# Stick-breaking attention: the scan's input moves from PSUM to SBUF, and the PSUM banks are dealt out anew

## The chip, the cores and the metric

The kernel runs on one core of a Trainium2 chip. The metric is the device time of one execution in microseconds (us). TensorE (PE) multiplies matrices and writes PSUM, which has eight banks of 128 partitions x 512 fp32 values; VectorE (DVE), ScalarE (ACT) and GpSimd (POOL) work element by element; SyncE (SP) issues most of the DMAs. Each engine takes its instructions in the order in which they were written.

## The reference

One decoder block for 2048 tokens of width 1024: conditioning, a projection, eight attention heads of 64 channels beside four pooling groups, an output projection and a feed-forward layer. The change lies in the attention:

```python
z = q @ k.T / sqrt(64)                     # scores, strictly causal (s < t)
logw[t, s] = logsigmoid(z[t, s]) + sum_{s < j < t} logsigmoid(-z[t, j])
out = exp(logw) @ v
```

The kernel doesn't form logarithms. The weight of key s is sigmoid(z_s) times the product of sigmoid(-z_j) over the later keys j, so each row of scores needs two sigmoids and one running product from right to left.

## The kernel before, in words

The kernel has four stages on the time axis of the profile: conditioning and input projection (to about 325 us), attention (about 325 to 862 us, with the rest of the input projection woven in), output projection with the second norm (to about 1060 us), and the feed-forward layer. Engine orders of the first two stages are written out by hand: the order of the calls in the source is the order in each engine's queue.

**The steps of the attention.** The work goes by units (h, tb, sc): head h, a block of 512 queries tb, a block of 512 keys sc, from sc = tb (the diagonal block) down to 0. A unit has four steps, i = 0 to 3, each with 128 queries on the partitions and L keys along the free axis: L = 512 off the diagonal, 128, 256, 384 and 512 on it. There are 80 units and 320 steps: 192 off the diagonal, and 128 on it. In pass n of the main loop the engines get, in this order:

- `weights_step` of step n (L792 to 808). PE puts the scores into a PSUM bank z (L801, L802, and L804 for the mask). ACT writes sigmoid(z) to an SBUF tile sg (L806), and then sigmoid(-z) over the scores in the same PSUM bank (L807).
- `scan_step` of step n-1 (L810 to 823). POOL writes the column at the right end of an SBUF tile pr: 1.0 on the diagonal (L815), else column 0 of the pr of the same i in the unit before (L817). DVE runs the scan from right to left (L818): first input z in PSUM, second input sg (with operation bypass, so that its values don't count), start value the same column of the older pr. POOL multiplies sg by pr shifted by one key and gets the weights w (L821).
- `values_step` (L839 to 855): two products of turned weights with values, into a PSUM bank av.
- `turn_step` of step n-7 (L825 to 838). PE turns four 128x128 blocks of w into a PSUM bank wt (L833); ACT rounds it to wth (L59), DVE subtracts for the rest wtl (L60).
- some pieces of the remaining projection (`pieces`): three products of 512 columns each and now and then an eviction, a split of weights by ACT and POOL, a running sum by POOL.

**Buffers.** PSUM has three banks z, two wt, two av and one mm (for the woven projection). In SBUF pr has 6 buffers (four of them hold the start values of the next unit), sg 5, w 11. `z_ps`, `t_ps`, `av_ps` hand out the banks (L153 to 155), each group in turn.

Of the kernel before, what the change touches and what calls it, by code (L numbers as in the profile page):

```python
# [9 lines left out]
F32 = mybir.dt.float32  # L10
F32R = mybir.dt.float32r
AF = mybir.ActivationFunctionType
ALU = mybir.AluOpType
# [4 lines left out]
P = 128  # L18
# [10 lines left out]
TB = 512  # L29
# [3 lines left out]
NEG = -1e30  # L33
LAG = 2
OFF = 7
ZB, WB = 3, 2
FT = {"sr": 4, "p1": 1, "u2": 2, "u3": 2, "u4": 1, "cu": 2, "s": 6, "gs": 3, "tr": 4, "gf": 1}
PAIRS, HELD = 6, 4
RB = PAIRS - 1
# [5 lines left out]
def block_kernel(ctx, tc, x, c, w_cond, b_cond, g_mix_pre, g_mix_post, w_in, w_pool,  # L45
                 pool_scale, w_out, g_ffn_pre, g_ffn_post, w_gate, w_up, w_down, out):
    nc = tc.nc
# [17 lines left out]
    def mm3(ps, terms, first=True, last=True):  # L65

        n = len(terms)
        for i, ((lh, ll), (rh, rl)) in enumerate(terms):
            nc.tensor.matmul(ps, lh, rh, start=first and i == 0, stop=False)  # L69
            nc.tensor.matmul(ps, lh, rl, start=False, stop=False)  # L70
            nc.tensor.matmul(ps, ll, rh, start=False, stop=last and i == n - 1)  # L71

    def open_pool(stack, name, bufs=1, side=None):
        kw = {"side": side} if side else {}
        return stack.enter_context(tc.tile_pool(name=name, bufs=bufs, reuse_waits="tile", **kw))
# [68 lines left out]
    def psum(tag, bufs, name):  # L144
        return psp.tile([P, TB], F32, tag=tag, bufs=bufs, name=name)

    turn = [0]

    def mm_ps(name, alone=False):
        turn[0] += 1  # L150
        return z_ps(name) if turn[0] % 2 and not alone else psum("mm", 1, name)

    z_ps = lambda name: psum("z", ZB, name)  # L153
    t_ps = lambda name: psum("wt", WB, name)
    av_ps = lambda name: psum("av", 2, name)

    ident_r = c1.tile([P, P], F32R, tag="ident_r", name="ident_r")
    nc.vector.tensor_copy(ident_r, ident)
# [2 lines left out]
    one = ones[:, 0:1]  # L161
# [149 lines left out]
    def tokens(tb, k, cols=slice(0, TB)):  # L311
        if tb == 1:
            both = ht[1][k // HK]
            return both[:, 0, k % HK, cols], both[:, 1, k % HK, cols]
        return ht[tb][0][:, k, cols], ht[tb][1][:, k, cols]
# [111 lines left out]
    def pieces(th, chunks, tasks, loaded):  # L427
# [11 lines left out]
        for i, (n, tb) in enumerate(tasks):  # L439
            kind, m = chunks[n]  # L440
            ps = mm_ps(f"{kind}{m}_{tb}", attending)
            for k in range(KC):
                if k == 0 and th and todo.get(KC * i, [(0, 0)])[0][1] is None:
                    loaded[todo[KC * i][0][0]] = chunk_load(chunks[todo[KC * i][0][0]], th)
                    todo[KC * i].pop(0)
                w = loaded[n]
                mm3(ps, [((w[1][:, k, :], w[2][:, k, :]), tokens(tb, k))],
                    first=k == 0, last=k == KC - 1)
                for c, part in todo.get(KC * i + k, ()):
                    if part is None:  # L450
                        loaded[c] = chunk_load(chunks[c], th)
                    else:
                        chunk_split(loaded[c], part)
                if k == KC - 1:
                    take_chunk(chunks[n], tb, ps)
                run_small()
                yield
            if th == 1:
                yield

    def take_chunk(chunk, tb, ps):
        kind, m = chunk
        if kind == "u":
            ops = pool_ops(tb, ps, m)
            urgent.append(next(ops))
            small.append(ops)
        else:
            urgent.append(lambda: store_qk(tb, ps, (qd if kind == "q" else kd)[m], f"{kind}{m}"))

    def v_pieces(wvs, pool):  # L470
        for tb in (1, 0, 2, 3):
            for j in range(4):
                ps = mm_ps(f"v{tb}_{j}")
                cols = slice(j * P, (j + 1) * P)
                for k in range(KC):
                    mm3(ps, [(tokens(tb, k, cols), (wvs[0][:, k, :], wvs[1][:, k, :]))],
                        first=k == 0, last=k == KC - 1)
                    if k == KC - 1:
                        urgent.append(lambda a=(tb, j, ps, pool): store_v(*a))
                    run_small()  # L480
                    yield
# [119 lines left out]
        modulate(1, kc, pt)  # L601

    first_ps = {}
    first_banks = {(0, 0): ("mm", 1), (0, 1): ("av", 2), (1, 1): ("av", 2)}

    def first_products(n, tb, *ks):
        if (n, tb) not in first_ps:
            first_ps[n, tb] = psum(*first_banks.get((n, tb), ("z", ZB)), f"first{n}_{tb}")
        ps = first_ps[n, tb]
        for k in ks:  # L610
            mm3(ps, [((loaded[n][1][:, k, :], loaded[n][2][:, k, :]), tokens(tb, k))], first=k == 0, last=k == KC - 1)
        if ks[-1] == KC - 1:
            take_chunk(chunks[n], tb, ps)
# [15 lines left out]
    chunk_split(loaded[0], 3)  # L629
    modulate0(0, 1)  # L630
    first_products(0, 0, 0, 1)
    scales = [normed_rows(1, 0, early1[0]), normed_rows(1, 1, early1[1])]
    chunk_split(loaded[1], 0)
    chunk_split(loaded[1], 1)
    modulate0(2, 3)
    scales += [normed_rows(1, 2, early1[2]), normed_rows(1, 3, early1[3])]
    first_products(1, 0, 0, 1)
    first_products(0, 0, 2, 3)
    chunk_split(loaded[1], 2)
    chunk_split(loaded[1], 3)  # L640
# [129 lines left out]
    att = open_pool(ph1, "att", bufs=2)  # L770
# [14 lines left out]
        nc.sync.dma_start(raw(vt), vd[tb][:, h, :].rearrange("(b p) e -> p b e", p=P))  # L785
        return qt

    qts, prevs, avs, wss = {}, {}, {}, {}

    scans = []  # L790

    def weights_step(u, i):  # L792

        h, tb, sc = u
        diag = sc == tb
        kt, qt = kv[h, sc][0], qts[h, tb]
        L = (i + 1) * P if diag else TB
        nm = f"{h}_{tb}_{sc}_{i}"
        z = z_ps(f"z{nm}")
        keys = kt[:, 0:L]  # L800
        nc.tensor.matmul(z[:, 0:L], qt[:, 0, i * P:(i + 1) * P], keys, start=True, stop=False)  # L801
        nc.tensor.matmul(z[:, 0:L], qt[:, 1, i * P:(i + 1) * P], keys, start=False, stop=not diag)  # L802
        if diag:
            nc.tensor.matmul(z[:, i * P:L], ident_r, neg_r, start=False, stop=True)  # L804
        sg = att.tile([P, TB], F32, tag="sg", bufs=5, name=f"sg{nm}")
        nc.scalar.activation(sg[:, 0:L], z[:, 0:L], AF.Sigmoid, scale=0.125)  # L806
        nc.scalar.activation(z[:, 0:L], z[:, 0:L], AF.Sigmoid, scale=-0.125)  # L807
        scans.append((u, i, z, sg, L, nm))

    def scan_step(u, i, z, sg, L, nm):  # L810

        diag = u[1] == u[2]
        pr = att.tile([P, TB + 1], F32, tag="pr", bufs=6, name=f"pr{nm}")
        if diag:
            nc.gpsimd.memset(pr[:, L:L + 1], 1.0)  # L815
        else:
            nc.gpsimd.tensor_copy(pr[:, L:L + 1], prevs[i][:, 0:1])  # L817
        nc.vector.tensor_tensor_scan(pr[:, 0:L][:, ::-1], z[:, 0:L][:, ::-1], sg[:, 0:L],  # L818
                                     one if diag else prevs[i][:, 0:1], ALU.mult, ALU.bypass)
        w = att.tile([P, TB], F32, tag="w", bufs=OFF + 4, name=f"w{nm}")  # L820
        nc.gpsimd.tensor_tensor(w[:, 0:L], sg[:, 0:L], pr[:, 1:L + 1], ALU.mult)  # L821
        prevs[i] = pr
        wss.setdefault(u, []).append(w)

    def turn_step(u, b):  # L825
# [58 lines left out]
        next(fill)  # L884
    taken = START
    attending = True
    steps = [(u, i) for u in units for i in range(4)]

    def wo_load():
# [5 lines left out]

    SEQUENCE = [sb * NT // 2 + half * 4 + i for sb in range(2) for i in range(4) for half in range(2)]
    mixed = {}
    banks = itertools.cycle([("z", ZB)] * ZB + [("mm", 1)] + [("wt", WB)] * WB + [("av", 2)] * 2)
    f_ps = lambda name: psum(*next(banks), name)

    def mix_load(T):
        tb, cols = T // 4, slice((T % 4) * P, (T % 4 + 1) * P)
# [50 lines left out]
    for n in range(len(steps) + OFF):  # L953
        if n < len(steps):
            u, i = steps[n]
            if i == 0:
                unit_loads(u)
            weights_step(u, i)
            spent += 2.5 if u[1] == u[2] else 4.0
        if len(scans) > 1 or n >= len(steps) and scans:  # L960
            scan_step(*scans.pop(0))
        if len(waiting) > LAG:
            values_step(*waiting.pop(0))
        if n >= OFF:
            u, b = steps[n - OFF]
# [606 lines left out]
```

## Time and profile before

| | |
|---|---|
| time, median of 3 runs | 2353.0 us (2349.61 to 2356.45) |
| profiled execution, its own time | 2351.43 us |
| its span, first to last instruction | 2349.6 us |
| mean granted TensorE clock | 0.991 |
| PE, DVE, ACT, POOL busy, share of the span | 97%, 70%, 50%, 55% |
| first and last scan start | 326.0 and 860.3 us |

The span is 1.8 us shorter than the execution. In rows of groups, `pr<-z,pr,sg` names the output and the inputs of the instructions; `128x512` is partitions by elements. An instruction's duration runs from its start to its end, a time in which it waits inside the engine included; what it waited before its start stands in the idle column.

### The profile page before, as it was taken

Reading aid. Unit: us, or ns where it says so; the run is one execution under the profiler, and the core shown is the slowest. Engines: PE = TensorE matmul, PEld = TensorE weight load, DVE = VectorE, ACT = ScalarE, POOL = GpSimd, SP = SyncE. Lnnn points to the kernel's source line nnn. Section 1 sums busy time; section 2 is a strip of 40 time slices with the busy share of each in tenths; the row PEclk is TensorE's granted clock in tenths of the full one; section 3 lists DMA queues with packets and bytes.
Section 4 is the critical chain, followed back from the end, with each engine's and each line's share of the span. In section 5 each row is a group of like instructions: output and inputs, shape, how many; then the busy total and the mean of one; then the engine's idle time right before and its main releaser. Section 6 shows DMA issues by size and latency. Waiting matters only on the chain.

```text
span 2349.6 us, 33532 instructions
## 1 busy us (share of the span) xinstructions
PE 2278.4 (97%) x10717; PEld 1866.6 (79%) x10717; DVE 1638.0 (70%) x2221; ACT 1179.3 (50%) x2411; POOL 1293.3 (55%) x1429
## 2 busy tenths in 40 slices
PE   6999999999999989999999999999999999999997
PEld 3778878888888768887888888788888888888885
DVE  6764549999999975757565565886776565555556
ACT  4323659899998864444222232454533323234444
POOL 4542337787677764544777778430475665641004
PEclk9999999999999999999999999999999999999998
DMA  8785764333443636656554555776763333327554
GB/s 287 244 293 193 273 189 117 90 105 90 126 113 95 190 99 196 220 193 203 163 167 153 162 161 179 264 243 201 257 196 101 119 110 95 114 86 279 193 196 144
DMA packets 307116, 405.18 MB, mean 172 GB/s; under 512 B 19254, under 2 KB 179578, under 8 KB 303868
## 3 DMA queue, kind: packets, MB, share of 16 engines
q1 hardware_dynamic: 302620, 400.68, 52.8%
q10 hardware_dynamic: 4320, 2.36, 0.4%
q8 instruction: 85, 1.39, 0.2%
q14 instruction: 91, 0.75, 0.1%
HBM read 274.51 MB, written 128.45 MB: 171 GB/s over the span
## 4 chain that ended last, share of the span: by engine, by line
PE 79%; DVE 7%; issue 4%; ACT 4%; POOL 3%; DMA 3%; SPq 0%; DVEq 0%; POOLq 0%; ACTq 0%
PE t_u L70 3%; PE t_u L69 3%; PE t_u L71 3%; PE t_g L70 3%; PE t_g L69 3%; PE t_g L71 3%; PE wt L833 3%; PE dn0p L70 3%; PE dn0p L71 3%; PE dn0p L69 3%; PE dn1p L70 3%; PE dn1p L69 3%; PE dn1p L71 3%; DVE pr L818 3%; PE b_g L70 2%
## 5 line engine op out<-in xcount | busy, mean ns | idle before, releaser
L821 POOL TENSOR_TENSOR w<-sg,pr 128x512 f32<-128x512 f32 (+2 forms) x320 | 306.1, 956 | 143.6 <-DVE pr L818 81.3
L1179 POOL TENSOR_TENSOR s<-s,cu 128x512 f32<-128x512 f32 x88 | 132.7, 1515 | 240.7 <-DVE cu L1178 140.1
L818 DVE TENSOR_TENSOR_SCAN pr<-z,pr,sg 128x512 f32<-128x512 f32 x192 | 244.5, 1274 | 0.5 <-POOL pr L817 0.5
L60 DVE TENSOR_TENSOR wtl<-wt,wth 128x512 fp32r<-128x512 f32 (+1 forms) x320 | 190.3, 595 | 35.0 <-ACT wth L59 33.0
L806 ACT ACTIVATE sg<-z 128x512 f32<-128x512 f32 (+2 forms) x320 | 175.0, 547 | 48.0 <-PE z L804 22.2
L59 ACT CAST wth<-wt 128x512 fp32r<-128x512 f32 (+1 forms) x320 | 173.1, 541 | 21.5 <-PE wt L833 19.8
L833 PE MATMUL wt<-ident,w 128*128 128x128 f32 x1088 | 172.0, 273 | 2.5 <-DVE wtl L60 2.2
L807 ACT ACTIVATE z<-z 128x512 f32<-128x512 f32 (+2 forms) x320 | 174.1, 544 | 0.0
L60 DVE TENSOR_TENSOR u_s_l<-u_s,u_s_h 128x512 fp32r<-128x512 f32 x66 | 66.4, 1007 | 151.9 <-ACT u_s_h L59 151.9
L833 PEld LDWEIGHTS wt<-ident,w 128*128 128x128 f32 x1088 | 133.5, 140 | 32.6 <-DVE wtl L60 3.7
L1169 ACT ACTIVATE s<-s 128x512 f32<-128x512 f32 x88 | 55.7, 633 | 192.6 <-DVE s L1168 192.6
L801 PE MATMUL z<-kt,qt 128*128 128x512 f32 (+2 forms) x320 | 128.8, 403 | 16.8 <-DVE pr L818 12.2
L70 PE MATMUL dn0p<-w0p_l,g0p_h 128*128 128x512 f32 x308 | 121.2, 394 | 1.9 <-DVE w0p_l L60 1.9
L848 PE MATMUL av<-wth,vt 128*128 128x512 f32 (+1 forms) x320 | 121.5, 380 | 0.0
L60 DVE TENSOR_TENSOR u_a_l<-u,u_a_h 128x512 fp32r<-128x512 f32 x66 | 77.4, 1175 | 62.3 <-ACT u_a_h L59 62.3
L69 PE MATMUL dn0p<-w0p_h,g0p_h 128*128 128x512 f32 x308 | 120.5, 391 | 0.0
L71 PE MATMUL dn0p<-w0p_h,g0p_l 128*128 128x512 f32 x308 | 120.4, 391 | 0.0
L59 ACT CAST g_s_h<-g_s 128x512 fp32r<-128x512 f32 x66 | 39.5, 620 | 157.6 <-POOL g_s L1111 81.5
L849 PE MATMUL av<-wtl,vt 128*128 128x512 f32 (+1 forms) x320 | 116.9, 365 | 0.0
L802 PE MATMUL z<-kt,qt 128*128 128x512 f32 (+2 forms) x320 | 116.7, 365 | 0.0
L59 ACT CAST u_s_h<-u_s 128x512 fp32r<-128x512 f32 x66 | 38.6, 614 | 152.2 <-POOL u_s L1111 152.2
L70 PE MATMUL dn1p<-w1p_l,g1p_h 128*128 128x512 f32 x292 | 114.4, 392 | 0.0
(655 smaller groups left out, 7266.2 us busy)
## 6 DMA issues: line engine op xcount, KB each, us to landing
g<-in_w_gate_dram SPq DMA_DIRECT2D x42, 512.0 KB, 4.6
u<-in_w_up_dram SPq DMA_DIRECT2D x42, 512.0 KB, 5.0
wc<-in_w_cond_dram SPq DMA_DIRECT2D x32, 512.0 KB, 5.8
qt<-qd SPq DMA_DIRECT2D x64, 256.0 KB, 3.9
wd<-in_w_down_dram SPq DMA_DIRECT2D x44, 256.0 KB, 3.0
tdt<-wd SPq DMA_DIRECT2D x44, 256.0 KB, 2.0
w0p<-tdt SPq DMA_DIRECT2D x44, 256.0 KB, 2.9
w1p<-tdt SPq DMA_DIRECT2D x44, 256.0 KB, 2.8
```

The source lines that it names most:

```text
L59: nc.scalar.copy(hi, src)
L60: low.tensor_tensor(lo, src, raw(hi), ALU.subtract)
L69: nc.tensor.matmul(ps, lh, rh, start=first and i == 0, stop=False)
L70: nc.tensor.matmul(ps, lh, rl, start=False, stop=False)
L71: nc.tensor.matmul(ps, ll, rh, start=False, stop=last and i == n - 1)
L801: nc.tensor.matmul(z[:, 0:L], qt[:, 0, i * P:(i + 1) * P], keys, start=True, stop=False)
L806: nc.scalar.activation(sg[:, 0:L], z[:, 0:L], AF.Sigmoid, scale=0.125)
L807: nc.scalar.activation(z[:, 0:L], z[:, 0:L], AF.Sigmoid, scale=-0.125)
L818: nc.vector.tensor_tensor_scan(pr[:, 0:L][:, ::-1], z[:, 0:L][:, ::-1], sg[:, 0:L], one if diag else prevs[i][:, 0:1], ALU.mult, ALU.bypass)
L821: nc.gpsimd.tensor_tensor(w[:, 0:L], sg[:, 0:L], pr[:, 1:L + 1], ALU.mult)
L833: nc.tensor.transpose(wt[:, i * P:(i + 1) * P], wss[u][i][:, b * P:(b + 1) * P], ident)
L1179: nc.gpsimd.tensor_tensor(s, s, u, ALU.mult)
```

## The change

The second sigmoid is written to the tile pr in SBUF, which is now taken in `weights_step` and not in `scan_step`. The scan reads pr and writes over it. The start values of the next unit no longer stay in the older pr: after each scan but those of the last key block (sc = 0) POOL copies column 0 to a small tile `carry`, 192 copies in all. PSUM tags are one bank each, dealt out by `bank_cycle`. Before the attention and after it the groups stand as before; in the attention z has two banks and wt has three.

```diff
-    z_ps = lambda name: psum("z", ZB, name)
-    t_ps = lambda name: psum("wt", WB, name)
-    av_ps = lambda name: psum("av", 2, name)
+    def bank_cycle(*tags):
+        tags = itertools.cycle(tags)
+        return lambda name: psum(next(tags), 1, name)
+
+    z_ps, t_ps, av_ps, mm_only = bank_cycle("z0", "z1", "z2"), bank_cycle("w0", "w1"), bank_cycle("a0", "a1"), bank_cycle("mm")
...
         nc.scalar.activation(sg[:, 0:L], z[:, 0:L], AF.Sigmoid, scale=0.125)
-        nc.scalar.activation(z[:, 0:L], z[:, 0:L], AF.Sigmoid, scale=-0.125)
-        scans.append((u, i, z, sg, L, nm))
+        pr = att.tile([P, TB + 1], F32, tag="pr", bufs=PRB, name=f"pr{nm}")
+        nc.scalar.activation(pr[:, 0:L], z[:, 0:L], AF.Sigmoid, scale=-0.125)
+        scans.append((u, i, pr, sg, L, nm))
...
-        pr = att.tile([P, TB + 1], F32, tag="pr", bufs=6, name=f"pr{nm}")
-        if diag:
+        carry = carries.pop(i, None)
+        if carry is None:
             nc.gpsimd.memset(pr[:, L:L + 1], 1.0)
         else:
-            nc.gpsimd.tensor_copy(pr[:, L:L + 1], prevs[i][:, 0:1])
-        nc.vector.tensor_tensor_scan(pr[:, 0:L][:, ::-1], z[:, 0:L][:, ::-1], sg[:, 0:L],
-                                     one if diag else prevs[i][:, 0:1], ALU.mult, ALU.bypass)
+            nc.gpsimd.tensor_copy(pr[:, L:L + 1], carry)
+        nc.vector.tensor_tensor_scan(pr[:, 0:L][:, ::-1], pr[:, 0:L][:, ::-1], sg[:, 0:L],
+                                     one if carry is None else carry, ALU.mult, ALU.bypass)
+        if u[2]:
+            carries[i] = att.tile([P, 1], F32, tag=f"carry{i}", bufs=2, name=f"carry{nm}")
+            nc.gpsimd.tensor_copy(carries[i], pr[:, 0:1])
         w = att.tile([P, TB], F32, tag="w", bufs=OFF + 4, name=f"w{nm}")
         nc.gpsimd.tensor_tensor(w[:, 0:L], sg[:, 0:L], pr[:, 1:L + 1], ALU.mult)
-        prevs[i] = pr
...
     attending = True
+    z_ps, t_ps, av_ps, mm_only = bank_cycle(*('z0', 'z1')), bank_cycle(*('w0', 'w1', 'z2')), bank_cycle(*('a0', 'a1')), bank_cycle(*('mm',))
...
-    banks = itertools.cycle([("z", ZB)] * ZB + [("mm", 1)] + [("wt", WB)] * WB + [("av", 2)] * 2)
-    f_ps = lambda name: psum(*next(banks), name)
+    f_ps = bank_cycle("z0", "z1", "z2", "mm", "w0", "w1", "a0", "a1")
```

`PRB` is 6, so pr keeps its 6 buffers. The instruction orders of PE, DVE and ACT are the same in both kernels; POOL's differs by the 192 copies, each between the scan's end and the multiplication of its step.

More of the change, by code (lines that the diff above doesn't have):

```diff
@@ L35 @@
 OFF = 7
-ZB, WB = 3, 2
+PRB = 6
 FT = {"sr": 4, "p1": 1, "u2": 2, "u3": 2, "u4": 1, "cu": 2, "s": 6, "gs": 3, "tr": 4, "gf": 1}
@@ L150, in mm_ps @@
         turn[0] += 1
-        return z_ps(name) if turn[0] % 2 and not alone else psum("mm", 1, name)
-    z_ps = lambda name: psum("z", ZB, name)
-    t_ps = lambda name: psum("wt", WB, name)
-    av_ps = lambda name: psum("av", 2, name)
+        return z_ps(name) if turn[0] % 2 and not alone else mm_only(name)
+    def bank_cycle(*tags):
+        tags = itertools.cycle(tags)
+        return lambda name: psum(next(tags), 1, name)
+    z_ps, t_ps, av_ps, mm_only = bank_cycle("z0", "z1", "z2"), bank_cycle("w0", "w1"), bank_cycle("a0", "a1"), bank_cycle("mm")
     ident_r = c1.tile([P, P], F32R, tag="ident_r", name="ident_r")
@@ L603, in block_kernel @@
     first_ps = {}
-    first_banks = {(0, 0): ("mm", 1), (0, 1): ("av", 2), (1, 1): ("av", 2)}
+    first_banks = {(0, 0): mm_only, (0, 1): av_ps, (1, 1): av_ps}
     def first_products(n, tb, *ks):
         if (n, tb) not in first_ps:
-            first_ps[n, tb] = psum(*first_banks.get((n, tb), ("z", ZB)), f"first{n}_{tb}")
+            first_ps[n, tb] = first_banks.get((n, tb), z_ps)(f"first{n}_{tb}")
         ps = first_ps[n, tb]
@@ L786, in block_loads @@
         return qt
-    qts, prevs, avs, wss = {}, {}, {}, {}
+    qts, carries, avs, wss = {}, {}, {}, {}
     scans = []
@@ L806, in weights_step, with scan_step @@
         nc.scalar.activation(sg[:, 0:L], z[:, 0:L], AF.Sigmoid, scale=0.125)
-        nc.scalar.activation(z[:, 0:L], z[:, 0:L], AF.Sigmoid, scale=-0.125)
-        scans.append((u, i, z, sg, L, nm))
-    def scan_step(u, i, z, sg, L, nm):
+        pr = att.tile([P, TB + 1], F32, tag="pr", bufs=PRB, name=f"pr{nm}")
+        nc.scalar.activation(pr[:, 0:L], z[:, 0:L], AF.Sigmoid, scale=-0.125)
+        scans.append((u, i, pr, sg, L, nm))
+    def scan_step(u, i, pr, sg, L, nm):
         diag = u[1] == u[2]
-        pr = att.tile([P, TB + 1], F32, tag="pr", bufs=6, name=f"pr{nm}")
-        if diag:
+        carry = carries.pop(i, None)
+        if carry is None:
             nc.gpsimd.memset(pr[:, L:L + 1], 1.0)
         else:
-            nc.gpsimd.tensor_copy(pr[:, L:L + 1], prevs[i][:, 0:1])
-        nc.vector.tensor_tensor_scan(pr[:, 0:L][:, ::-1], z[:, 0:L][:, ::-1], sg[:, 0:L],
-                                     one if diag else prevs[i][:, 0:1], ALU.mult, ALU.bypass)
+            nc.gpsimd.tensor_copy(pr[:, L:L + 1], carry)
[4 more added lines that the diff above has]
+            nc.gpsimd.tensor_copy(carries[i], pr[:, 0:1])
         w = att.tile([P, TB], F32, tag="w", bufs=OFF + 4, name=f"w{nm}")
         nc.gpsimd.tensor_tensor(w[:, 0:L], sg[:, 0:L], pr[:, 1:L + 1], ALU.mult)
-        prevs[i] = pr
         wss.setdefault(u, []).append(w)
```

## The prediction, made before the result was known

> **What bounds the kernel now.** I read the page first, for the stages, then a table of stretches for the attention, because the change touches nothing else.
>
> ```profile
> span 2349.6 us, 33532 instructions
> PE   6999999999999989999999999999999999999997
> DVE  6764549999999975757565565886776565555556
> POOL 4542337787677764544777778430475665641004
> PEclk9999999999999999999999999999999999999998
> ```
>
> Each digit is 58.7 us of the span. PE is full from end to end; DVE is at 9 only in digits 7 to 14, which is the attention. The stretches give it in microseconds:
>
> ```profile
> core 0: us, PE busy (x) PEld busy (x) DVE busy (x) ACT busy (x) POOL busy (x), PEclk, DMA share, GB/s
> 50.00:60.00 10.00, 5.30 (x25) 4.70 (x23) 6.87 (x8) 0.00 (x0) 2.91 (x2) 0.78 0.33 105
> 60.00:70.00 10.00, 10.00 (x35) 7.98 (x35) 6.16 (x10) 4.33 (x7) 4.73 (x4) 0.71 0.41 133
> 70.00:80.00 10.00, 10.00 (x51) 8.29 (x50) 5.78 (x9) 4.12 (x7) 2.60 (x2) 1.00 0.55 199
> 325.00:862.00 537.00, 517.62 (x2944) 427.99 (x2943) 508.53 (x649) 478.82 (x1054) 394.60 (x715) 1.00 0.41 119
> 842.00:854.00 12.00, 10.34 (x55) 7.57 (x53) 12.00 (x15) 11.20 (x24) 9.49 (x16) 1.00 0.18 44
> ```
>
> In the 537 us of the attention DVE is busy for 508.5 and PE for 517.6, so both are near their limit; POOL is idle for 537 - 394.6 = 142.4 us. In the last stretch, without woven projection, DVE is busy for all 12 us. Its beat can be read from the timeline there:
>
> ```profile
> 841.27 1.28 DVE L818 TENSOR_TENSOR_SCAN pr<-z,pr,sg 128x512 f32<-128x512 f32 x1
> 842.46 0.67 DVE L60 TENSOR_TENSOR wtl<-wt,wth 128x512 fp32r<-128x512 f32 x1
> 842.72 1.09 POOL L821 TENSOR_TENSOR w<-sg,pr 128x512 f32<-128x512 f32 x1 [0.55 <-DVE pr L818]
> 843.04 1.27 DVE L818 TENSOR_TENSOR_SCAN pr<-z,pr,sg 128x512 f32<-128x512 f32 x1
> ```
>
> One full step is scan and subtraction, 843.04 - 841.27 = 1.77 us. The row to remember is POOL's: its w (842.72 to 843.81) runs beside the next scan (from 843.04), and neither is lengthened. So it goes through the whole stage:
>
> ```profile
> L818 DVE TENSOR_TENSOR_SCAN pr<-z,pr,sg x192: 1267/1274/1282, 335.8 to 860.3; 128x512 f32<-128x512 f32 x192
> L821 POOL TENSOR_TENSOR w<-sg,pr x320: 407/1091/1105, 326.7 to 862.5; 128x512 f32<-128x512 f32 x96, 128x128 f32<-128x128 f32 x32, 128x384 f32<-128x384 f32 x32
> L817 POOL COPY pr<-pr x192: 173/184/647, 336.6 to 862.2; 128x1 f32<-128x1 f32 x192
> ```
>
> (minimum, median and maximum in ns). 192 scans differ by 15 ns in all.
>
> **The change, part 1: the scan's first input.** Before, the scan reads one tensor from PSUM (z) and one from SBUF (sg). After, it reads both from SBUF (pr, sg). Does that matter? No scan of before has two SBUF inputs, but other DVE instructions have, in the feed-forward stage, beside POOL multiplications that read SBUF too:
>
> ```profile
> 1148.96 1.18 DVE L60 TENSOR_TENSOR g_s_l<-g_s,g_s_h 128x512 fp32r<-128x512 f32 x1
> 1149.56 1.74 POOL L1179 TENSOR_TENSOR s<-s,cu 128x512 f32<-128x512 f32 x1
> 1150.07 1.77 DVE L60 TENSOR_TENSOR u_a_l<-u,u_a_h 128x512 fp32r<-128x512 f32 x1
> 1153.08 1.29 POOL L1187 TENSOR_TENSOR s<-s,s 128x512 f32<-128x512 f32 x1
> 854.65 2.13 DVE L60 TENSOR_TENSOR ml<-m,mh 128x512 fp32r<-128x512 f32 x2
> 855.58 0.65 POOL L817 COPY pr<-pr 128x1 f32<-128x1 f32 x1
> L60 DVE TENSOR_TENSOR ml<-m,mh x32: 678/686/1783, 854.6 to 1040.5; 128x512 fp32r<-128x512 f32 x32
> ```
>
> The POOL row of 1.29 us, and the 678 ns minimum of ml, are such instructions undisturbed. The others take turns. POOL begins at 1149.56, but ends at 1151.30, which is 1.16 us after DVE's first one ended (1150.14): it had waited for that. DVE's second begins at 1150.07 and ends at 1151.84, 0.54 us after POOL's end: it had waited too. A DVE instruction with two SBUF inputs and a POOL instruction that reads SBUF exclude each other for their whole length; only some 0.12 to 0.14 us (1.29 - 1.16, 0.678 - 0.54) are saved at each change of turn. The 647 ns of the one-column copy (184 ns at the median) are the same in the attention: it stands beside the two ml at 854.65. The subtraction wtl, with one input in PSUM, shows none of it.
>
> In the Trainium skill, SBUF — State Buffer, section Who interferes with whom, says that a DVE instruction with two SBUF inputs contends with a GpSimd instruction that reads SBUF, and that the loser blocks fully. The rows above agree for two-input subtractions; no row shows a scan in that case. By that rule a scan waits as they do; without it the sum would be that of the first rival below.
>
> I take it that the scan behaves as the subtractions do, since the second tensor input is what the disturbed rows have and the undisturbed ones lack. Then the time of the stage is bounded by what scans and POOL's reading instructions need together. The scans:
>
> ```profile
> L818 DVE TENSOR_TENSOR_SCAN pr<-z,pr,sg 128x512 f32<-128x512 f32 x192 | 244.5, 1274 | 0.5 <-POOL pr L817 0.5
> L818 DVE TENSOR_TENSOR_SCAN pr<-z,ones,sg 128x512 f32<-128x512 f32 x32 | 40.8, 1274 | 0.5 <-ACT z L807 0.5
> L818 DVE TENSOR_TENSOR_SCAN pr<-z,ones,sg 128x384 f32<-128x384 f32 x32 | 32.2, 1007 | 0.8 <-POOL pr L815 0.8
> L818 DVE TENSOR_TENSOR_SCAN pr<-z,ones,sg 128x256 f32<-128x256 f32 x32 | 23.6, 739 | 0.0
> L818 DVE TENSOR_TENSOR_SCAN pr<-z,ones,sg 128x128 f32<-128x128 f32 x32 | 15.1, 473 | 0.0
> L815 POOL MEMSET pr<- 128x1 f32 x127 | 12.6, 99 | 0.0
> L817 POOL COPY pr<-pr 128x1 f32<-128x1 f32 x191 | 35.7, 187 | 0.0
> ```
>
> They sum to 244.5 + 40.8 + 32.2 + 23.6 + 15.1 = 356.2 us. A scan's own length from SBUF is unknown; the subtractions take 678 ns from SBUF and 670 from PSUM (the timeline's wtl), so I leave it, with 320 x 0.01 = 3 us either way. POOL reads SBUF for 394.6 - 12.6 (memsets, which read nothing) = 382.0 us.
>
> **Part 2: the 192 carry copies.** Each is a one-column copy, 187 ns: 192 x 0.187 = 35.9 us on POOL, between the scan and the w of its step. Were there no exclusion, POOL's 142.4 idle us would hide them: w is turned seven steps later. With it they count. The scan's new wait on a carry is for the copy of four steps ago, which POOL has long made before the w of that step: nothing. Claims together: 356.2 + 382.0 + 35.9 = 774.1 us, against 537.
>
> What lessens and what adds: two changes of turn a step save 320 x (0.12 + 0.14) = 83 us at most, giving 691. Where POOL is not behind, it starts only 0.17 us after the scan's end (842.72 against 841.27 + 1.28), a time in which nobody reads: 320 x 0.17 = 54 us, giving 745; without the savings 774 + 54 = 828 is the far end. DVE's subtraction fits under POOL's w (0.67 against 1.09). I take 740, near the 745 of a POOL that keeps step, because each w needs the scan just ended: 740 - 537 = **+203 us**. As a check by one full step: 1.27 - 0.13 for the scan, 0.17 until POOL, 0.19 for the carry, 1.09 for w are 2.59 us in place of 1.77.
>
> **Part 3: the second sigmoid's place.** ACT writes SBUF in place of PSUM, both from PSUM:
>
> ```profile
> L806 ACT ACTIVATE sg<-z 128x512 f32<-128x512 f32 x224 | 137.0, 611 | 30.4 <-PE z L802 18.6 <-PE z L804 6.6 <-POOL pr L815 1.4
> L807 ACT ACTIVATE z<-z 128x512 f32<-128x512 f32 x224 | 136.3, 609 | 0.0
> ACT sg L806 <- POOL w L821: 1.2, 3, 0.5
> PE z L801 <- DVE pr L818: 12.2, 30, 1.1
> PE wt L833 <- DVE wtl L60: 2.2, 1, 2.2
> PEld z L801 <- DVE pr L818: 1.3, 1, 1.3
> PEld wt L833 <- DVE wtl L60: 3.7, 4, 2.7
> ```
>
> 611 against 609 ns: 320 x 0.002 = 0.6 us, nothing. It adds a wait: ACT needs a pr buffer that w and carry of six steps ago have left. Behind it on ACT stand wth and the evictions of the projection, and PE waits for those. But the first sigmoid waits already for an sg buffer that w of five steps ago has left (1.2 us in 3 times), which is stricter. Nothing.
>
> **Part 4: the banks.** A z bank is free after its second sigmoid and not after its scan, but there are two and not three; wt gets the third. At most the waits shown go: 12.2 + 1.3 for the scan, 2.2 + 3.7 for wtl, 19.4 us. Under the exclusion they are worth nothing, since PE then waits for w. The new wait, for ACT two steps back, has a step of 1.77 us against two sigmoids of 0.61: nothing. Before and after the attention the banks go round as they did: nothing.
>
> **Sum.** 2351.4 (the profiled execution) + 203 = 2554; that execution is 1.6 us under the median of 2353.0, so **2556 us**.
>
> **The rivals.**
> *The scan doesn't exclude POOL* (the other side). Its operation ignores the values of sg, and the chip may not fetch them through the path that POOL needs. For it: no scan in the trace is ever disturbed; against it: sg is a tensor input like the others. It decides if scans stay at 1274 ns beside w. Then carries are hidden, and of the 19.4 us that PE waits only the part goes that DVE, which has 537 - 508.5 = 28.5 us idle, doesn't give back. I take 13: 2353 - 13 = 2340, between 2330 and 2356.
> *Half an exclusion*: only one of the two waits, or scans find gaps in POOL's work. About half the price, +100: 2453, between 2420 and 2500.
> *The clock drops as well.* In the rows above a stretch with PE at 5.30 of 10 us is granted 0.78, then 0.71. With 740 us PE would be busy for some 517.6/740 = 70%, in parts less. Against it: 842 to 854, with gaps in each step, is granted 1.00, and a slower PE is busier: at 70 us the clock is full again. I allow +60: 2616, to 2680. The Trainium skill, TensorE: Matmul & The Clock Gate, Part 1, has the clock at half after an idle window of about 3.4 us; the first rows fit that, and no step here would idle so long.
>
> **Chances.** Full exclusion 0.72 (2500 to 2645, from the ends 691 and 828), half 0.10, clock 0.04, none 0.14. The likeliest is 2556. From 2420 to 2650 lie the first but for its edges, the second and half of the third: 0.82. Faster by over 0.3% (7 us, about what a measurement here tells from no change): 0.10 of the 0.14; within 0.3%: 0.04; slower: 0.86.
>
> **What would show it.** In the profile of after: scans with a spread from 1.27 to about 2.4 us (1.27 + 1.09), w from 1.09 to about 2.3, and their busy times together near the length of a stage of about 740 us; PE and ACT waiting on w and pr. Wrong if 128x512 scans stay within 15 ns; too large if scan and w overlap in the timeline; part 2 wrong if carries run in POOL's idle time. The stages before 325 us and behind the attention should keep their lengths to a few us.

## The result and the profile after

The kernel after takes 2501.7 us (median of 4 runs, 2496.5 to 2505.7) against 2354.7 us in the same comparison: 1.0626 times the time before, 95% interval 1.0599 to 1.0654. Its profiled execution took 2500.74 us, with a span of 2499.0. The page of the kernel after, its slices as before (one digit is now 62.5 us):

```profile
span 2499.0 us, 33374 instructions
PE   6999988888988887999999999999999999999997
DVE  6674489998999989466756566588676556565556
POOL 4542278999899999455477877842056665562004
PEclk9999999998999988999999999999999999999998
```

In digits 6 to 16 PE stands at 8 or 7 but for one digit, and POOL at 9 from digit 8 on but for one. A wait inside an instruction counts as busy, so these digits of POOL and DVE hold waits as well as work. The stretches of the kernel after show the attention, now from 325 to 1009 us, and the rest of the kernel (length, busy time of PE, PEld, DVE, ACT and POOL, granted clock, then the DMA figures):

```profile
325.00:1009.00 684.00, 572.34 (x2932) 460.49 (x2933) 635.24 (x649) 479.83 (x1051) 634.05 (x906) 0.92 0.33 93
1009.00:2499.00 1490.00, 1466.63 (x6477) 1204.83 (x6475) 940.96 (x1290) 570.79 (x1089) 774.74 (x564) 0.99 0.53 173
```

The attention lasts 684 us in place of 537, which is 147 of the 149 us by which the span grew; what follows takes 1490 us against 1488 (2350 - 862). The groups of the scan and of POOL, and the waits of that stretch, in the kernel after (line, engine, operation, output and inputs, count, then busy us and mean ns; a wait is total us, times, longest):

```profile
L821 DVE TENSOR_TENSOR_SCAN pr<-pr,carry,sg x192: 1269/1729/2206, 334.4 to 1006.0; 128x512 f32<-128x512 f32 x192
L827 POOL TENSOR_TENSOR w<-sg,pr 128x512 f32<-128x512 f32 x223 | 259.5, 1164 | 11.4 <-DVE pr L821 3.2 <-PE av L853 0.2 <-DVE wtl L60 0.2
L820 POOL COPY pr<-carry 128x1 f32<-128x1 f32 x191 | 159.8, 837 | 0.0
L825 POOL COPY carry<-pr 128x1 f32<-128x1 f32 x192 | 67.5, 352 | 33.9 <-DVE pr L821 26.2 <-ACT wth L59 2.3 <-ACT pr L810 1.9
PEld wt L838 <- POOL w L827: 71.5, 51, 4.0
PE wt L838 <- POOL w L827: 58.7, 33, 3.8
ACT sg L808 <- POOL w L827: 53.4, 59, 3.8
```

The scan of 512 keys, which took 1267 to 1282 ns before, now takes 1269 to 2206. A copy of one column, 187 ns on average before (L817), takes 837. PE and ACT wait for w. The turns can be read in the timeline of the kernel after (start us, length us):

```profile
987.26 1.09 POOL L827 TENSOR_TENSOR w<-sg,pr 128x512 f32<-128x512 f32 x1
987.50 1.93 DVE L821 TENSOR_TENSOR_SCAN pr<-pr,carry,sg 128x512 f32<-128x512 f32 x1
988.30 1.12 POOL L820 COPY pr<-carry 128x1 f32<-128x1 f32 x1
989.56 0.18 POOL L825 COPY carry<-pr 128x1 f32<-128x1 f32 x1
989.70 1.09 POOL L827 TENSOR_TENSOR w<-sg,pr 128x512 f32<-128x512 f32 x1
989.80 2.07 DVE L821 TENSOR_TENSOR_SCAN pr<-pr,carry,sg 128x512 f32<-128x512 f32 x1
```

The first w ends at 988.35. The scan had started at 987.50, but ends at 989.43, 1.08 us after w: it stood still beside w and then ran. The end copy came at 988.30, beside the scan, and ends at 989.42, with it. The next scan ends at 991.87, again 1.08 us after its w (990.79). From the end of one scan to the end of the next it is 2.44 us; before, a step took 1.77.

### The profile page after: what moved, and what is told of

It is laid out like the page before. It is cut to its first block, busy times and chain, and to the rows that moved or that the text cites. A ratio compares the mean times of both kernels' runs of the same rounds, so it can differ in the third digit from the quotient of the medians.

```text
span 2499.0 us, 33374 instructions
## 1 busy us (share of the span) xinstructions
PE 2334.8 (93%) x10717; PEld 1900.9 (76%) x10717; DVE 1761.5 (70%) x2221; ACT 1183.0 (47%) x2411; POOL 1534.0 (61%) x1621
## 4 chain that ended last, share of the span: by engine, by line
PE 64%; DVE 17%; POOL 8%; issue 5%; DMA 2%; ACT 2%; SPq 1%; POOLq 0%; DVEq 0%; ACTq 0%
DVE pr L821 10%; DVE wtl L60 3%; PE t_u L69 3%; PE t_u L70 3%; PE t_u L71 3%; PE t_g L70 3%; PE t_g L69 3%; PE t_g L71 3%; PE dn0p L70 3%; PE dn0p L71 3%; PE dn0p L69 3%; PE dn1p L70 2%; PE dn1p L69 2%; PE dn1p L71 2%; PE b_g L70 2%
## 5 line engine op out<-in xcount | busy, mean ns | idle before, releaser
L827 POOL TENSOR_TENSOR w<-sg,pr 128x512 f32<-128x512 f32 (+2 forms) x320 | 330.1, 1032 | 18.3 <-ACT pr L810 3.2
L821 DVE TENSOR_TENSOR_SCAN pr<-pr,carry,sg 128x512 f32<-128x512 f32 x192 | 334.8, 1744 | 1.2 <-POOL carry L825 1.2
L838 PE MATMUL wt<-ident,w 128*128 128x128 f32 x1088 | 200.5, 292 | 87.6 <-POOL w L827 58.7
L838 PEld LDWEIGHTS wt<-ident,w 128*128 128x128 f32 x1088 | 145.7, 148 | 133.0 <-POOL w L827 71.5
L810 ACT ACTIVATE pr<-z 128x512 f32<-128x512 f32 (+2 forms) x320 | 174.5, 545 | 0.0
L820 POOL COPY pr<-carry 128x1 f32<-128x1 f32 x192 | 160.0, 833 | 0.0
L821 DVE TENSOR_TENSOR_SCAN pr<-pr,ones,sg 128x128 f32<-128x128 f32 (+3 forms) x128 | 151.8, 1190 | 0.0
L854 PE MATMUL av<-wtl,vt 128*128 128x512 f32 (+1 forms) x320 | 128.8, 403 | 20.1 <-DVE wtl L60 19.6
L803 PE MATMUL z<-kt,qt 128*128 128x512 f32 (+2 forms) x320 | 134.7, 421 | 2.3 <-ACT pr L810 2.3
L853 PE MATMUL av<-wth,vt 128*128 128x512 f32 (+1 forms) x320 | 127.7, 399 | 0.0
L804 PE MATMUL z<-kt,qt 128*128 128x512 f32 (+2 forms) x320 | 122.2, 382 | 0.0
```

Of the source, the lines that this page charges most:

```text
L810: nc.scalar.activation(pr[:, 0:L], z[:, 0:L], AF.Sigmoid, scale=-0.125)
L820: nc.gpsimd.tensor_copy(pr[:, L:L + 1], carry)
L821: nc.vector.tensor_tensor_scan(pr[:, 0:L][:, ::-1], pr[:, 0:L][:, ::-1], sg[:, 0:L], one if carry is None else carry, ALU.mult, ALU.bypass)
L838: nc.tensor.transpose(wt[:, i * P:(i + 1) * P], wss[u][i][:, b * P:(b + 1) * P], ident)
```

## The experiments

The theory: the scan with two SBUF inputs and POOL's reads of SBUF exclude each other, and the sum of both, less what is saved at each change of turn, sets the length of the stage. The rivals: the SBUF write of the second sigmoid, the carry copies, the two score banks, the lower clock.

**One SBUF input again, all else kept (e1).** Banks as before the change.

```diff
-    z_ps, t_ps, av_ps, mm_only = bank_cycle(*('z0', 'z1')), bank_cycle(*('w0', 'w1', 'z2')), bank_cycle(*('a0', 'a1')), bank_cycle(*('mm',))
+    z_ps, t_ps, av_ps, mm_only = bank_cycle(*('z0', 'z1', 'z2')), bank_cycle(*('w0', 'w1')), bank_cycle(*('a0', 'a1')), bank_cycle(*('mm',))
...
-        nc.vector.tensor_tensor_scan(pr[:, 0:L][:, ::-1], pr[:, 0:L][:, ::-1], sg[:, 0:L],
+        nc.vector.tensor_tensor_scan(pr[:, 0:L][:, ::-1], pr[:, 0:L][:, ::-1], z[:, 0:L],
```

> The kernel after with two edits: the scan's second input (whose values the operation ignores) is the score bank z in PSUM in place of sg in SBUF, and, since z is now held until the scan, z has three banks and wt two, as before the change. The second sigmoid still goes to SBUF, the scan still works in place in pr, the 192 carry copies are still made. Exclusion theory (two SBUF inputs of the scan against POOL's reads is the whole price): within 10 us of the kernel before, 2345 to 2365; 128x512 scans all near 1.27 us. Rival (the SBUF write of the sigmoid, the carry copies and the new waits carry the price): near the kernel after, 2480 to 2510.

Measured: 2349.7 us against 2351.9, ratio 0.9989 (0.9978 to 0.9999). In its profile the line of the scan has no spread left:

```profile
L821 DVE TENSOR_TENSOR_SCAN pr<-pr,carry,z x192: 1269/1271/1275, 331.5 to 852.6; 128x512 f32<-128x512 f32 x192
```

The second sigmoid in SBUF, the scan in place and the carries are all still there. The place of the second input, with the bank deal that this edit brings along, takes the whole price away; the next run separates the two.

**The banks alone (e2).** The kernel after, with three score banks and two for turned weights.

> The kernel after with the PSUM banks of before in the attention: three for scores, two for turned weights. Exclusion theory: no change against after (2502), 2492 to 2512, since PE waits for w and not for a bank. Rival (two score banks make PE and ACT wait and are part of the 147 us): 2400 to 2480.

Measured: 2498.3 us, ratio to before 1.0616 (1.0595 to 1.0637), which can't be told from the kernel after. The bank deal is neither price nor gain there.

**The carries alone (e3).** The kernel before, with

```diff
+            nc.gpsimd.tensor_copy(pr[:, L:L + 1], carry)
...
+                                     one if carry is None else carry, ALU.mult, ALU.bypass)
+        if u[2]:
+            carries[i] = att.tile([P, 1], F32, tag=f"carry{i}", bufs=2, name=f"carry{nm}")
+            nc.gpsimd.tensor_copy(carries[i], pr[:, 0:1])
```

> The kernel before with the carry copies alone: 192 one-column copies by POOL, the scan starts from them; second sigmoid and scan input stay in PSUM. Exclusion theory: hidden in POOL's 142 us of idle time, 2350 to 2360 (up to 5 us slower). Rival (the copy delays w and so the turn): 192 x 0.2 to 0.26 us, 2390 to 2405.

Measured: 2351.0 us, ratio 0.9999 (0.9989 to 1.0009). Without the exclusion POOL's idle time hides them.

**One SBUF input with two score banks (e7).** As e1, with the banks of after.

> The kernel after with the scan's second input taken from the score bank z in PSUM, with the banks of after: two for scores, three for turned weights. There is no exclusion, but the score bank is held until the scan with only two of them. Exclusion theory: scans at 1.27 us; PE waits more for z, at most some 0.3 us a step more than with three banks: 2360 to 2450. Rival (the price is elsewhere): near 2500 or above.

Measured: 2489.6 us, ratio 1.0587 (1.0570 to 1.0603): the expected range was too low, by 40 us. Its scans are undisturbed, and its waits are others:

```profile
L821 DVE TENSOR_TENSOR_SCAN pr<-pr,carry,z x192: 1269/1271/1274, 338.2 to 1000.7; 128x512 f32<-128x512 f32 x192
PEld z L803 <- DVE pr L821: 127.5, 156, 2.3
PE z L803 <- DVE pr L821: 111.2, 155, 2.0
```

Here a score bank is held through product, two sigmoids and scan, and there are only two. I had allowed 0.3 us a step for that (about 100 us); it was (2489.6 - 2349.7) / 320 = 0.44. So two score banks do here only where the second sigmoid frees them, and with two of them the kernel after does need that sigmoid in SBUF.

**Less reading by POOL (e4, e5, e6).** Three runs for the size of the price, with reads taken from the kernel after: e4 leaves out half of each w, e5 the end copies, e6 the carries and with them the end copies.

```diff
# e4
-        nc.gpsimd.tensor_tensor(w[:, 0:L], sg[:, 0:L], pr[:, 1:L + 1], ALU.mult)
+        nc.gpsimd.tensor_tensor(w[:, 0:L // 2], sg[:, 0:L // 2], pr[:, 1:L // 2 + 1], ALU.mult)
+        nc.gpsimd.memset(w[:, L // 2:L], 0.01)
# e5
-            nc.gpsimd.tensor_copy(pr[:, L:L + 1], carry)
+            nc.gpsimd.memset(pr[:, L:L + 1], 1.0)
# e6
-        if u[2]:
+        if False:
             carries[i] = att.tile([P, 1], F32, tag=f"carry{i}", bufs=2, name=f"carry{nm}")
```

> The kernel after; POOL multiplies only the left half of each w, and fills the right half with a constant (left out: half of the weights). A memset reads nothing. POOL's reading time falls by about 224 x 0.45 + 32 x (0.35 + 0.23 + 0.11) = 123 us. Exclusion theory (the stage lasts as long as scans and POOL's reads together): the time falls from 2502 by most of it, to 2370 to 2410; the floor is the kernel before, 2352. Rival (the price is the longer chain of one step, or the lower clock, and not the sum): 2440 to 2500.

> The kernel after with a memset in place of the 192 copies into the end column of pr (left out: the product carried into that column). The memset reads nothing. The prediction counted these copies at 0.187 us each, 36 us: 2502 - 36 = 2466. The trace of after says that they wait through the scan and end with it, so that they cost nothing: 2495 to 2505.

> The kernel after without the carry copies, so that every scan starts from 1.0 and every end column is a memset (left out: the product carried between key blocks). Neither one-column copy is left. By the prediction's sum 2 x 36 us less: 2430. By the trace of after, in which a carry puts w off by 0.14 us between two scans: 192 x 0.14 = 27 us less, 2475; if the carry hides as well: 2495 to 2505.

Measured: e4 2397.6 us, ratio 1.0192 (1.0171 to 1.0214); e5 2469.3, ratio 1.0509 (1.0494 to 1.0525); e6 2454.7, ratio 1.0441 (1.0425 to 1.0456). Half of the w, 123 us of reading, is worth 104 us, though the memsets in its place keep POOL busy for 89 us: the time follows POOL's reads, and not all of its work. The end copies are worth 32 us, though most end together with a scan; I had expected nothing after reading the timeline, and the prediction's 36 us was near. In e5 the memset goes through beside a running scan, and w takes the copy's place in the line:

```profile
701.77 1.94 DVE L821 TENSOR_TENSOR_SCAN pr<-pr,carry,sg 128x512 f32<-128x512 f32 x1
702.57 0.10 POOL L820 MEMSET pr<- 128x1 f32 x1
L827 POOL TENSOR_TENSOR w<-sg,pr 128x512 f32<-128x512 f32 x223 | 296.0, 1328 | 16.4 <-DVE pr L821 7.3 <-ACT pr L810 1.2 <-PE av L853 0.2
```

A w of 1328 ns on average in place of 1164 is one that more often stands ready behind a scan and starts at once when the scan lets go, where it would else come a copy later. That is my reading; no run tests it alone, but a count in the traces agrees: 84 w of e5 last over 0.1 us longer than the shortest of their shape, and 32 of the kernel after. The carries are worth 15 us more (2469.3 - 2454.7), less than half of the 36 predicted and about half of the 27 expected from the timeline.

**A second input of one column (e8).**

```diff
-        nc.vector.tensor_tensor_scan(pr[:, 0:L][:, ::-1], pr[:, 0:L][:, ::-1], sg[:, 0:L],
+        nc.vector.tensor_tensor_scan(pr[:, 0:L][:, ::-1], pr[:, 0:L][:, ::-1], one.to_broadcast([P, L]),
```

> The kernel after with the scan's second input taken from a single SBUF column of ones, read again for each key (128x512 with step 0), in place of sg. If the exclusion goes by the kind of the operand (a second tensor read from SBUF, however small), nothing changes: 2495 to 2510. If it goes by the data fetched: near the kernel before, 2352.

Measured: 2501.0 us, ratio 1.0643 (1.0627 to 1.0659), the kernel after. In these runs it doesn't matter which tile the second input is or how little data stands behind it, only that it is read from SBUF.

**The clock (e9).**

```diff
-        for i in range(i0, 4):
+        for i in [*range(i0, 4)] * 2:
             nc.tensor.transpose(wt[:, i * P:(i + 1) * P], wss[u][i][:, b * P:(b + 1) * P], ident)
```

> The kernel after with each block of w turned twice into the same place of the bank (a second, useless set of 1088 products of 128 columns on PE), to keep PE busier through the gaps. PE's clock was granted at 0.92 in the attention of after, against 1.00 before. If the lower clock is part of the 147 us: the granted clock rises and the time falls below 2490. Exclusion theory (the stage lasts as long as scans and POOL's reads): the clock rises towards 1 and the time stays, 2495 to 2515, since 4 x 0.1 us more of PE a step fit into a step of over 2 us.

Measured: 2508.4 us, ratio 1.0672 (1.0656 to 1.0688). The stretch of the attention in its profile (behind the busy times of the five engines stands the granted clock):

```profile
325.00:1013.00 688.00, 638.68 (x3999) 553.96 (x4000) 630.55 (x649) 489.79 (x1052) 633.15 (x906) 0.98 0.32 93
```

The granted clock rises from 0.92 to 0.98, and the stage lasts 688 us in place of 684. A higher clock brings nothing back. A gain cancelled by the added work isn't excluded by this run alone; but scans and POOL's reads cover 664 of the 684 us in the kernel after (counted below), which leaves little room for the clock.

**What the change was after, without the exclusion (e10).** The scan's second input is one column of a PSUM bank, so that one SBUF input is left and the score bank is free after the second sigmoid. The bank comes from the turned weights.

```diff
-    z_ps, t_ps, av_ps, mm_only = bank_cycle(*('z0', 'z1')), bank_cycle(*('w0', 'w1', 'z2')), bank_cycle(*('a0', 'a1')), bank_cycle(*('mm',))
+    z_ps, t_ps, av_ps, mm_only = bank_cycle(*('z0', 'z1')), bank_cycle(*('w0', 'w1')), bank_cycle(*('a0', 'a1')), bank_cycle(*('mm',))
...
+    filler = psum('z2', 1, 'filler')
+    nc.vector.memset(filler[:, 0:1], 1.0)
...
-        nc.vector.tensor_tensor_scan(pr[:, 0:L][:, ::-1], pr[:, 0:L][:, ::-1], sg[:, 0:L],
+        nc.vector.tensor_tensor_scan(pr[:, 0:L][:, ::-1], pr[:, 0:L][:, ::-1], filler[:, 0:1].to_broadcast([P, L]),
```

> The kernel after with the scan's second input read from one constant column of a PSUM bank (step 0), and for that two banks for scores, two for turned weights and one for the constant. One SBUF input is left, and the score bank is free after the second sigmoid, as the change meant it. Exclusion theory: scans at 1.27 us, PE's waits for the scan (12 us) gone, DVE's own load the limit: 2335 to 2352. Rival (something else in the change costs as well): above 2360.

Measured: 2340.0 us against 2350.8, ratio 0.9951 (0.9938 to 0.9963): half a per cent faster than the kernel before, and faster than the kernel after. Its profile:

```profile
325.00:851.00 526.00, 513.35 (x2944) 425.61 (x2943) 503.32 (x648) 468.62 (x1056) 416.78 (x909) 1.00 0.43 122
L821 DVE TENSOR_TENSOR_SCAN pr<-pr,carry,filler x192: 1268/1273/1281, 335.7 to 850.2; 128x512 f32<-128x512 f32 x192
PE wt L838 <- DVE wtl L60: 8.7, 27, 1.8
PE z L803 <- ACT pr L810: 1.6, 4, 0.5
```

PE's 12.2 us of waiting for the scan are gone, 1.6 us of waiting for the second sigmoid have come, and 8.7 us for the bank of turned weights in place of 2.2. DVE is busy for 503 of 526 us and PE for 513, nearly full as both were before (509 and 518 of 537); which of the two sets the pace isn't shown. e8 and e10 each read one constant column, e8 from SBUF and e10 from PSUM, and differ beside that only in a third bank for turned weights: 2501.0 and 2340.0 us.

## Why the prediction was right, and where its sizes were off

**The mechanism was right.** The prediction put the whole price on the scan's second SBUF input; e1 against e2 shows it, e8 against e10 agrees, and most of the marks that it named came: a spread of the scans to 2.2 us (it said about 2.4), PE and ACT waiting for w, the rest of the kernel unchanged. One came only in part: w was to spread to about 2.3 us, but only 32 of 320 are lengthened (to 2.13 at most). It is mostly the end copy of the next step that stands behind the scan, 149 of 192 times. The page SBUF — State Buffer of the Trainium skill, section Who interferes with whom, holds for the scan as well, which no row of before could show; it also says that a GpSimd instruction which only writes doesn't contend, and the memset of 0.10 us beside a running scan in e5 agrees.

**The size was off: 203 us forecast, 147 measured (2556 against 2501.7).** Two terms of the sum failed, the savings and the idle time; the claims of 774 us were lessened by too little. Counted from every instruction in the trace of the kernel after, a scan or a reading instruction of POOL is under way in 664 of the 684 us. So 774 - 664 = 110 us were saved at changes of turn, where the prediction had "83 us at most", and for 20 us neither ran, where it had 54. That gives 664 + 20 = 684, where it had 691 + 54 = 745 and took 740.

The savings were too small because "only some 0.12 to 0.14 us are saved at each change of turn" was read from one POOL multiplication and one subtraction (1.29 - 1.16 is 0.13 there, and not 0.12). In the kernel after 259 scans and 281 reading instructions of POOL last over 0.1 us longer than the shortest of their shape, which makes 540 changes of turn with a wait: 110 / 540 = 0.20 us each. The scan behind w above gives 1.27 - 1.08 = 0.19, and the full step took 2.44 us, where the prediction's check had 2.59. The idle time was too large because 0.17 us was charged for each of 320 scans; the trace has 178 pauses in which neither runs, of 0.11 us on average. The time of 2501.7 us lies just inside the 2500 to 2645 given to full exclusion, and the stage of 684 us outside the 691 to 828 behind it.

The carries cost 15 us, where 36 were claimed. Counted in the same way (in e5 up to 978 us, in e6 up to 963.5), the run without carries saves 13 us less at changes of turn, and has 8 us more in which neither runs.

**Part 1**, the same scan length from SBUF: 1269 ns at least, right. **Part 2**, carries free without the exclusion: right (e3). **Part 3**, the second sigmoid's place: right (e1). **Part 4**, the banks worth nothing under the exclusion: right (e2); worth up to 19 us without it: e10 gained 11 (2350.8 - 2340.0), with one bank less than the change has.

**The rivals.** The first said 2340 for a scan that doesn't exclude POOL. e10 built a case like it, with one bank less, and took 2340.0; that the figures are the same is in part luck, since 13 us of gain from 2353 were forecast and 10.8 from 2350.8 measured. Against the clock rival stood that no step would idle for the window of about 3.4 us; that argument failed. The clock fell to 0.92, in most cases without a pause of PE as long as that (the last section shows it). Where this differs from the idle window that the prediction cites from the Trainium skill, TensorE: Matmul & The Clock Gate, Part 1, the measurement decides. A price of the lower clock was not found (e9).

## What to carry to other kernels

Before an operand of a DVE instruction is moved from PSUM to SBUF, count its SBUF tensor inputs: the step from one to two made the scan take turns with all that POOL reads here, and in 664 of the 684 us one of the two was running. An input whose values are ignored was an input all the same; read from one constant PSUM column with step 0 it didn't lengthen the scan (1268 to 1281 ns), but it takes a PSUM bank. The sign stood in the profile of before: instructions of one shape whose minimum and maximum lie far apart (ml, 678 to 1783 ns), beside others of the same engine that don't spread (the scan, 1267 to 1282). Such a spread can have other causes; what stands beside the long ones in the timeline tells.

## What the runs showed of the hardware that was not expected

An instruction that waits for its turn ends sooner after the other than its own length: a scan of 1.27 us 1.08 after w, a copy of 0.18 together with the scan. And who starts first doesn't always go first. Two rows of the kernel after:

```profile
992.11 2.21 DVE L821 TENSOR_TENSOR_SCAN pr<-pr,carry,sg 128x512 f32<-128x512 f32 x1
992.14 1.10 POOL L827 TENSOR_TENSOR w<-sg,pr 128x512 f32<-128x512 f32 x1
```

The scan starts 0.03 us before w, but w takes its usual time and ends at 993.24, and the scan ends at 994.32, again 1.08 us after it. So the turn isn't taken at the recorded start. Part of a scan, some 0.2 us, seems to be done before its turn; for the copy it may also be that the turn passes before the recorded end of the scan, which the rows don't say.

The granted clock fell to 0.92 with PE busy for 572 of 684 us, without a price that showed. In the trace of after it falls to a half 23 times in the attention, for 3.4 to 10.2 us. One such fall in the stretches of the kernel after:

```profile
368.61:372.02 3.41, 1.48 (x8) 0.97 (x7) 3.37 (x4) 1.52 (x3) 3.33 (x6) 1.00 0.24 77
372.02:375.43 3.41, 3.41 (x12) 2.73 (x11) 3.04 (x4) 1.77 (x4) 3.41 (x8) 0.50 0.01 2
```

In the first stretch PE is busy for 1.48 of 3.41 us, and its longest pause is 1.37 us; in the next the clock is halved, though PE is busy all through. Before each of the 23 falls PE had been busy for at most 58% of the 3.4 us ahead of it, and only three pauses of PE in the stage are longer than 3.4 us. In the attention of before, PE was busy for at least 60% of every such window, and the clock never fell.
